# Loads and stores of a log-softmax moved into one DMA queue, one whole tile in turns

## The chip, the cores and the metric

The kernel runs on one core of one Trainium2 chip. The metric is the device time of one execution in microseconds (us). Where this document speaks of packets, a "row" is a contiguous run of 50,000 bytes (a quarter of a row of the array), which is what one packet of a whole-tile transfer moves, and the "excess" is the time by which a packet is longer than the shortest usual one, 1847 ns.

## The reference

A log-softmax over the last axis of a float32 array of 16 x 512 x 50,000:

```python
max_x = np.max(x, axis=-1, keepdims=True)
shifted = x - max_x
log_sum_exp = np.log(np.sum(np.exp(shifted), axis=-1, keepdims=True))
return (shifted - log_sum_exp).astype(np.float32)
```

Every byte is read once and written once: 1638.4 MB each way.

## The kernel before

The 8192 rows of the array are cut into 256 tiles of 32 rows; a tile is 128 partitions of 12,500 floats (6.4 MB), four partitions to a row, and four buffers hold tiles in flight. SyncE issues the loads, ScalarE the stores, and each issuing engine owns one DMA queue. VectorE finds maxima and subtracts, ScalarE makes exponentials and their sums, and TensorE adds the sums of the four partitions of a row.

```python
    @block.sync                                   # loads
    def _(sync):
        ...
        load_parts(0, 0)                          # the first tile in four quarters
        for t in range(1, NBUF):
            load(t, xt[t])
        take(sync, stored[0], 16 * NS)
        load(0, xt[NBUF])
        src = run(xt, NBUF + 1, rounds - 1)
        with sync.Fori(0, rounds - 1) as q:
            for i in range(NBUF):
                j = (i + 1) % NBUF
                take(sync, stored[j])             # the buffer's store has landed
                load(j, src(q, i))
        ...
        load_parts(NBUF - 1, ntiles - 1)          # the last tile in quarters too

    @block.scalar                                 # exponentials, and the stores
    def _(scalar):
        ...
        def store(j, dst, buf):
            subtracted.next(scalar.dma_start(out=dst, in_=buf)).then_inc(stored[j], 16)

        def whole(j, dst):
            for c in range(NS):
                ...                               # exp of a quarter of the columns, with its sum
            ...
            log(j)
            store(j, dst, bufs[j])
```

Of the kernel before, what the change touches and what calls it, by code (L numbers as in the profile page):

```python
# [19 lines left out]
NBUF = 4  # L20

NS = 4
# [27 lines left out]
def cols(c):  # L50
    return slice(c * C, (c + 1) * C)
# [3 lines left out]
def kernel(  # L55
# [12 lines left out]

    rounds = (ntiles - NBUF) // NBUF
    assert ntiles % NBUF == 0 and rounds >= 2  # L70
    tail = range(1 + rounds * NBUF, ntiles - 1)

    xt = xf.rearrange("(t r) (g w) -> t (r g) w", r=R, g=G)
    ot = of.rearrange("(t r) (g w) -> t (r g) w", r=R, g=G)
# [63 lines left out]
    def _(gpsimd):  # L138
        k = 0
        for g in (GS, G):  # L140
# [10 lines left out]
            ).wait_op(ready, k + 2, "sem-ge").then_inc(ready)  # L151
            k += 3

    @block.sync
    def _(sync):
        def load(j, src):
            sync.dma_start(out=bufs[j], in_=src).then_inc(landed[j], 16)

        def load_parts(j, t):
            for s in range(NS):  # L160
                sync.dma_start(out=bufs[j][:, cols(s)], in_=xs[t, s]).then_inc(
                    landed_part[s], 16
                )

        load_parts(0, 0)
        for t in range(1, NBUF):
            load(t, xt[t])
        take(sync, stored[0], 16 * NS)
        load(0, xt[NBUF])
        src = run(xt, NBUF + 1, rounds - 1)  # L170
        with sync.Fori(0, rounds - 1) as q:
            for i in range(NBUF):
                j = (i + 1) % NBUF
                take(sync, stored[j])
                load(j, src(q, i))
        for t in tail:
            take(sync, stored[t % NBUF])
            load(t % NBUF, xt[t])
        take(sync, stored[NBUF - 1])
        load_parts(NBUF - 1, ntiles - 1)  # L180
        for j in range(NBUF - 1):
            take(sync, stored[j])
        take(sync, stored[NBUF - 1], 16 * NS)

    @block.vector
    def _(vector):
        def share(k, g, op, negate):

            on_dve.next(
                vector.transpose(out=allneg, in_=negp.to_broadcast([P, SQ]))  # L190
            ).then_inc(on_dve.sem)
            on_dve.next(
                vector.tensor_reduce(  # L193
                    out=rowneg[:, : SQ // g],
                    in_=allneg.rearrange("p (r g) -> p r g", g=g),
                    op=op, axis=AX, negate=negate,
                )
            ).then_inc(on_dve.sem)
            on_dve.next(
                vector.tensor_copy(  # L200
                    out=spread.rearrange("p (r g) -> p r g", g=g),
                    in_=rowneg[:, : SQ // g, None].to_broadcast([P, SQ // g, g]),
                )
            ).then_inc(on_dve.sem)
            on_dve.next(
                vector.transpose(out=negmaxs[k], in_=spread)  # L206
            ).then_inc(agreed.sem)

        def subtract(k, buf):
            logged.next(  # L210
                vector.tensor_scalar(  # L211
                    out=buf, in0=buf, scalar1=negmaxs[k][:, 0:1], scalar2=logs[k],
                    op0=ALU.add, op1=ALU.subtract,
                )
            ).then_inc(subtracted.sem)

        def whole(j):
            take(vector, landed[j])

            for c in range(NS):  # L220
                vector.tensor_reduce(  # L221
                    out=negms[j][:, c : c + 1], in_=bufs[j][:, cols(c)],
                    op=ALU.max, axis=AX, negate=True,
                ).then_inc(shifted.sem if c < NS - 1 else on_dve.sem)
            on_dve.next(vector.nop()).then_inc(shifted.sem)  # L225
            vector.tensor_reduce(  # L226
                out=negp, in_=negms[j], op=ALU.min, axis=AX
            ).then_inc(on_dve.sem)
            share(j, G, ALU.min, False)

            rescaled.next(
                vector.tensor_mul(out=scaleds[j], in0=scales[j], in1=parts[j])  # L232
            ).then_inc(summed.sem)
            subtract(j, bufs[j])

        def in_parts(j):
            for s in range(NS):
                take(vector, landed_part[s])
                vector.reduce_max(  # L239
                    out=negp, in_=bufs[j][:, cols(s)], axis=AX  # L240
                ).then_inc(on_dve.sem)
                share(NBUF + s, GS, ALU.max, True)
                if s:
                    subtract(NBUF + s - 1, bufs[j][:, cols(s - 1)])
            subtract(NBUF + NS - 1, bufs[j][:, cols(NS - 1)])

        def settle():
            for count in (on_dve, rescaled, logged):
                count.settle(vector)

        in_parts(0)
        settle()
        with vector.Fori(0, rounds):
            for i in range(NBUF):
                whole((i + 1) % NBUF)
            settle()
        for t in tail:
            whole(t % NBUF)
        in_parts(NBUF - 1)

    @block.scalar
    def _(scalar):
        def log(k):
            added.next(
                scalar.activation(out=logs[k], in_=rowsums[k], func=ACT.Ln)  # L265
            ).then_inc(logged.sem)

        def store(j, dst, buf):
            subtracted.next(scalar.dma_start(out=dst, in_=buf)).then_inc(stored[j], 16)

        def whole(j, dst):
            for c in range(NS):
                shifted.next(
                    scalar.activation(  # L274
                        out=dump, in_=bufs[j][:, cols(c)], func=ACT.Exp,
                        bias=negms[j][:, c : c + 1], scale=1.0,
                        accum_out=parts[j][:, c : c + 1],
                    )
                ).then_inc(on_act.sem)
                on_act.next(scalar.nop())  # L280
            agreed.next(
                scalar.activation(  # L282
                    out=scales[j], in_=negms[j], func=ACT.Exp,
                    bias=negmaxs[j][:, 0:1], scale=-1.0,
                )
            ).then_inc(rescaled.sem)
            log(j)
            store(j, dst, bufs[j])

        def in_parts(j, t):  # L290
            for s in range(NS):
                agreed.next(
                    scalar.activation(  # L293
                        out=dump, in_=bufs[j][:, cols(s)], func=ACT.Exp,
                        bias=negmaxs[NBUF + s][:, 0:1], scale=1.0,
                        accum_out=sub_sum[:, s : s + 1],
                    )
                ).then_inc(summed_part.sem)
                if s:
                    store(j, os[t, s - 1], bufs[j][:, cols(s - 1)])  # L300
                log(NBUF + s)
            store(j, os[t, NS - 1], bufs[j][:, cols(NS - 1)])

        def settle():
            for count in (on_act, shifted, agreed, added, subtracted):
                count.settle(scalar)

        nc.scalar.preload_act_table_set("natural_log_exp_and_others")  # L308
        in_parts(0, 0)
        settle()  # L310
        dst = run(ot, 1, rounds)
        with scalar.Fori(0, rounds) as q:
            for i in range(NBUF):
                whole((i + 1) % NBUF, dst(q, i))
            settle()
        for t in tail:
            whole(t % NBUF, ot[t])
        in_parts(NBUF - 1, ntiles - 1)

    @block.tensor  # L320
    def _(tensor):
        def whole(j):
            for c in range(NS):
                ins = tensor.matmul(  # L324
                    rowsums[j], ones[G], scaleds[j][:, c : c + 1],
                    start=c == 0, stop=c == NS - 1,
                )
                if c == 0:
                    summed.next(ins)
            ins.then_inc(added.sem)  # L330

        def in_parts():
            for s in range(NS):
                summed_part.next(
                    tensor.matmul(  # L335
                        rowsums[NBUF + s], ones[GS], sub_sum[:, s : s + 1],
                        start=True, stop=True,
                    )
                ).then_inc(added.sem)
            summed_part.settle(tensor)  # L340

        tensor.wait_ge(ready, 6)
        in_parts()
        with tensor.Fori(0, rounds):
            for i in range(NBUF):
                whole((i + 1) % NBUF)
            summed.settle(tensor)
        for t in tail:
            whole(t % NBUF)
        in_parts()  # L350


# [28 lines left out]
```

## Time and profile before

| | kernel before |
|---|---|
| time, median of the first 3 runs | 7594.52 us (7588.5 to 7618.48) |
| span of the profiled run | 7612.1 us |
| DMA queues | loads 50.2%, stores 49.8% of 16 engines |
| VectorE, ScalarE, TensorE busy | 72%, 42%, 6% |

The queue shares are the time that packets took on 16 DMA engines; they add up to the whole span. So transfers bind, and every microsecond must be looked for in the packets. The trace keeps a record of each packet (start, duration, size, queue, but not the engine's number). From these records come the packet means. The **trailing time** below comes from the landings that the trace keeps for each semaphore: a transfer ends with 16 of them, one per engine, and the trailing time is how much later the last one is than the median of the 16.

### The profile page before, as it was taken

To read this page: it belongs to the slowest core of one execution; us is meant where nothing else is said; L and a number is where in the kernel's file an instruction comes from. 1 tells how busy PE (TensorE), PEld (TensorE's weight loads), DVE (VectorE), ACT (ScalarE), POOL (GpSimd) and SP (SyncE) were. 2 spreads that over 40 slices of the span, in tenths; PEclk is the share of its full clock that TensorE was granted. 3 is DMA by queue.
4 is the path that set the end of the run, shared out by engine and by line. 5 is a ranking of instruction groups with operands and counts; after the bars stand their busy time and mean duration, and the time that the engine had idled before them with its cause. 6 is when DMAs were issued, how large, how long until landed. Compare 5 with 4: busy or idle time off the path is not lost. (4 is left out here: it accounts for less than half of the span.)

```text
span 7612.1 us, 14101 instructions
## 1 busy us (share of the span) xinstructions
PE 478.8 (6%) x2048; PEld 456.4 (6%) x2048; DVE 5445.7 (72%) x2842; ACT 3185.1 (42%) x2565; POOL 2.3 (0%) x10
## 2 busy tenths in 40 slices
PE   0000000000000000000000000000000000000000
PEld 0000000000000000000000000000000000000000
DVE  7777777777776777777767777777777777777777
ACT  4344444434444344443443444434434444344443
POOL 0000000000000000000000000000000000000000
DMA  9999999999999999999999999999999999999999
GB/s 423 434 433 433 434 434 434 433 433 434 434 433 432 432 432 431 431 432 428 429 429 429 426 427 429 431 430 432 432 431 431 433 433 433 434 433 431 432 433 393
DMA packets 75458, 3276.85 MB, mean 430 GB/s; under 512 B 8384, under 2 KB 8384, under 8 KB 8384
## 3 DMA queue, kind: packets, MB, share of 16 engines
q1 hardware_dynamic: 37728, 1638.42, 50.2%
q10 hardware_dynamic: 37728, 1638.42, 49.8%
q14 instruction: 2, 0.02, 0.0%
HBM read 1638.40 MB, written 1638.40 MB: 430 GB/s over the span
## 5 line engine op out<-in xcount | busy, mean ns | idle before, releaser
L274 ACT ACTIVATE dump<-buf,negm 128x3125 f32<-128x3125 f32 x1016 | 2914.3, 2868 | 3807.2 <-DVE negm L221 3710.5
L221 DVE TENSOR_REDUCE negm<-buf 128x1 f32<-128x3125 f32 x1016 | 3391.7, 3401 | 943.6 <-DVEq L47 943.6
L211 DVE TENSOR_SCALAR buf<-buf,negmax,logsum 128x12500 f32<-128x12500 f32 (+1 forms) x262 | 1739.7, 6640 | 553.9 <-ACT logsum L265 553.9
L324 PE MATMUL sums<-scaled,ones 128*128 128x1 f32 x2032 | 474.1, 355 | 7061.9 <-DVE scaled L232 7061.9
L324 PEld LDWEIGHTS sums<-scaled,ones 128*128 128x128 f32 x2032 | 452.4, 328 | 7083.6 <-DVE scaled L232 7083.6
L232 DVE TENSOR_TENSOR scaled<-scale,part 128x4 f32<-128x4 f32 x254 | 41.2, 162 | 575.4 <-ACT scale L282 575.4
L265 ACT ACTIVATE logsum<-sums 128x1 f32<-128x1 f32 x262 | 44.8, 171 | 552.3 <-PE sums L324 546.9
L274 ACT ACTIVATION_READ_ACCUMULATOR dump<-buf,negm 128x1 f32 x1016 | 189.4, 186 | 0.0
L282 ACT ACTIVATE scale<-negm,negmax 128x4 f32<-128x4 f32 x254 | 75.5, 297 | 23.5
L226 DVE TENSOR_REDUCE negp<-negm 128x1 f32<-128x4 f32 x254 | 39.9, 157 | 38.9 <-DVE negm L221 38.9
L206 DVE STREAM_TRANSPOSE negmax<-spread 128x32 f32<-128x32 f32 x262 | 55.5, 212 | 9.1
L190 DVE STREAM_TRANSPOSE allneg<-negp 128x32 f32<-128x32 f32 x262 | 55.4, 212 | 9.1
L193 DVE TENSOR_REDUCE rowneg<-allneg 128x8 f32<-128x32 f32 (+1 forms) x262 | 48.8, 186 | 9.1
L200 DVE COPY spread<-rowneg 128x32 f32<-128x32 f32 x262 | 47.5, 181 | 9.1
L293 ACT ACTIVATE dump<-buf,negmax 128x3125 f32<-128x3125 f32 x8 | 22.9, 2869 | 30.9 <-DVE negmax L206 30.9
L239 DVE TENSOR_REDUCE negp<-buf 128x1 f32<-128x3125 f32 x8 | 27.2, 3399 | 8.1 <-DVEq L47 8.1
L335 PE MATMUL sums<-sub_sum,ones 128*128 128x1 f32 x16 | 4.7, 363 | 59.0 <-ACT dump L293 59.0
L335 PEld LDWEIGHTS sums<-sub_sum,ones 128*128 128x128 f32 x16 | 4.0, 312 | 59.6 <-ACT dump L293 59.6
L308 ACT ACT_TABLE_LOAD x1 | 1.3, 1283 | 1.0 <-SPq L115 1.0
L293 ACT ACTIVATION_READ_ACCUMULATOR dump<-buf,negmax 128x1 f32 x8 | 1.5, 186 | 0.0
L144 POOL TENSOR_SCALAR_AFFINE_SELECT ones<-ones 128x128 f32<-128x128 f32 x2 | 0.9, 442 | 0.1
L148 POOL TENSOR_SCALAR_AFFINE_SELECT ones<-ones 128x128 f32<-128x128 f32 x2 | 0.9, 428 | 0.1
(5 smaller groups left out, 0.8 us busy)
## 6 DMA issues: line engine op xcount, KB each, us to landing
buf<-in_x_dram SPq DMA_DIRECT2D x254, 6250.0 KB, 39.9
out_dram<-buf ACTq DMA_DIRECT2D x254, 6250.0 KB, 52.6
buf<-in_x_dram SPq DMA_DIRECT2D x8, 1562.5 KB, 27.6
out_dram<-buf ACTq DMA_DIRECT2D x8, 1562.5 KB, 18.3
```

Source lines behind the costliest of these rows:

```text
L190: vector.transpose(out=allneg, in_=negp.to_broadcast([P, SQ]))
L193: vector.tensor_reduce(out=rowneg[:, : SQ // g], in_=allneg.rearrange("p (r g) -> p r g", g=g), op=op, axis=AX, negate=negate,)
L200: vector.tensor_copy(out=spread.rearrange("p (r g) -> p r g", g=g), in_=rowneg[:, : SQ // g, None].to_broadcast([P, SQ // g, g]),)
L206: vector.transpose(out=negmaxs[k], in_=spread)
L211: vector.tensor_scalar(out=buf, in0=buf, scalar1=negmaxs[k][:, 0:1], scalar2=logs[k], op0=ALU.add, op1=ALU.subtract,)
L221: vector.tensor_reduce(out=negms[j][:, c : c + 1], in_=bufs[j][:, cols(c)], op=ALU.max, axis=AX, negate=True,).then_inc(shifted.sem if c < ...
L226: vector.tensor_reduce(out=negp, in_=negms[j], op=ALU.min, axis=AX).then_inc(on_dve.sem)
L232: vector.tensor_mul(out=scaleds[j], in0=scales[j], in1=parts[j])
L265: scalar.activation(out=logs[k], in_=rowsums[k], func=ACT.Ln)
L274: scalar.activation(out=dump, in_=bufs[j][:, cols(c)], func=ACT.Exp, bias=negms[j][:, c : c + 1], scale=1.0, accum_out=parts[j][:, c : c + 1],
L282: scalar.activation(out=scales[j], in_=negms[j], func=ACT.Exp, bias=negmaxs[j][:, 0:1], scale=-1.0,)
L324: ins = tensor.matmul(rowsums[j], ones[G], scaleds[j][:, c : c + 1], start=c == 0, stop=c == NS - 1,)
```

## The change

The intent: one queue in place of two, so that the order of the transfers is the program's and no longer the engines' choice packet by packet. SyncE issues store t, waits until store t-1 has landed, and issues the load that reuses that buffer. The last tile, which came in quarters, is whole. The core of the diff:

```diff
-    tail = range(1 + rounds * NBUF, ntiles - 1)
+    tail = range(1 + rounds * NBUF, ntiles)
     ... (SyncE)
+        def store(t, dst):
+            j = t % NBUF
+            subtracted.next(sync.dma_start(out=dst, in_=bufs[j])).then_inc(stored[j], 16)
     ...
         with sync.Fori(0, rounds - 1) as q:
             for i in range(NBUF):
-                j = (i + 1) % NBUF
-                take(sync, stored[j])
-                load(j, src(q, i))
+                store(2 + i, dst(q, i))
+                take(sync, stored[(1 + i) % NBUF])
+                load(1 + i, src(q, i))
+            subtracted.settle(sync)
     ... (ScalarE)
-            store(j, dst, bufs[j])
     ... (VectorE, ScalarE and TensorE lose in_parts for the last tile)
```

More of the change, by code (lines that the diff above doesn't have):

```diff
@@ L155, in _, with load @@
     def _(sync):
-        def load(j, src):
+        def load(t, src):
+            j = t % NBUF
             sync.dma_start(out=bufs[j], in_=src).then_inc(landed[j], 16)
-        def load_parts(j, t):
-            for s in range(NS):
-                sync.dma_start(out=bufs[j][:, cols(s)], in_=xs[t, s]).then_inc(
-                    landed_part[s], 16
-                )
-        load_parts(0, 0)
+        def store(t, dst):
+            j = t % NBUF
+            subtracted.next(sync.dma_start(out=dst, in_=bufs[j])).then_inc(stored[j], 16)
+        for s in range(NS):
+            sync.dma_start(out=bufs[0][:, cols(s)], in_=xs[0, s]).then_inc(
+                landed_part[s], 16
+            )
         for t in range(1, NBUF):
             load(t, xt[t])
+        for s in range(NS):
+            subtracted.next(
+                sync.dma_start(out=os[0, s], in_=bufs[0][:, cols(s)])
+            ).then_inc(stored[0], 16)
+        store(1, ot[1])
         take(sync, stored[0], 16 * NS)
-        load(0, xt[NBUF])
-        src = run(xt, NBUF + 1, rounds - 1)
+        load(NBUF, xt[NBUF])
+        subtracted.settle(sync)
+        dst, src = run(ot, 2, rounds - 1), run(xt, NBUF + 1, rounds - 1)
         with sync.Fori(0, rounds - 1) as q:
             for i in range(NBUF):
-                j = (i + 1) % NBUF
-                take(sync, stored[j])
-                load(j, src(q, i))
-        for t in tail:
-            take(sync, stored[t % NBUF])
-            load(t % NBUF, xt[t])
-        take(sync, stored[NBUF - 1])
-        load_parts(NBUF - 1, ntiles - 1)
-        for j in range(NBUF - 1):
-            take(sync, stored[j])
-        take(sync, stored[NBUF - 1], 16 * NS)
+                store(2 + i, dst(q, i))
+                take(sync, stored[(1 + i) % NBUF])
+                load(1 + i, src(q, i))
+            subtracted.settle(sync)
+        for t in range(2 + NBUF * (rounds - 1), ntiles):
+            store(t, ot[t])
+            take(sync, stored[(t - 1) % NBUF])
+            if t + NBUF - 1 < ntiles:
+                load(t + NBUF - 1, xt[t + NBUF - 1])
+        take(sync, stored[(ntiles - 1) % NBUF])
     @block.vector
@@ L258, in _ @@
             whole(t % NBUF)
-        in_parts(NBUF - 1)
     @block.scalar
@@ L266, in log, with whole @@
             ).then_inc(logged.sem)
-        def store(j, dst, buf):
-            subtracted.next(scalar.dma_start(out=dst, in_=buf)).then_inc(stored[j], 16)
-        def whole(j, dst):
+        def whole(j):
             for c in range(NS):
@@ L287, in whole, with in_parts @@
             log(j)
-            store(j, dst, bufs[j])
-        def in_parts(j, t):
+        def in_parts(j):
             for s in range(NS):
@@ L298, in in_parts @@
                 ).then_inc(summed_part.sem)
-                if s:
-                    store(j, os[t, s - 1], bufs[j][:, cols(s - 1)])
                 log(NBUF + s)
-            store(j, os[t, NS - 1], bufs[j][:, cols(NS - 1)])
         def settle():
-            for count in (on_act, shifted, agreed, added, subtracted):
+            for count in (on_act, shifted, agreed, added):
                 count.settle(scalar)
         nc.scalar.preload_act_table_set("natural_log_exp_and_others")
-        in_parts(0, 0)
+        in_parts(0)
         settle()
-        dst = run(ot, 1, rounds)
-        with scalar.Fori(0, rounds) as q:
+        with scalar.Fori(0, rounds):
             for i in range(NBUF):
-                whole((i + 1) % NBUF, dst(q, i))
+                whole((i + 1) % NBUF)
             settle()
         for t in tail:
-            whole(t % NBUF, ot[t])
-        in_parts(NBUF - 1, ntiles - 1)
+            whole(t % NBUF)
     @block.tensor
@@ L349, in _ @@
             whole(t % NBUF)
-        in_parts()
 _INS = ['x']
```

## The prediction

> **What bounds the kernel now.** I read the page's DMA rows first, then its queue table, then the groups of instructions, and last the stretches of the trace at both ends of the run.
>
> ```profile
> DMA  9999999999999999999999999999999999999999
> GB/s 423 434 433 433 434 434 434 433 433 434 434 433 432 432 432 431 431 432 428 429 429 429 426 427 429 431 430 432 432 431 431 433 433 433 434 433 431 432 433 393
> DMA packets 75458, 3276.85 MB, mean 430 GB/s; under 512 B 8384, under 2 KB 8384, under 8 KB 8384
> q1 hardware_dynamic: 37728, 1638.42, 50.2%
> q10 hardware_dynamic: 37728, 1638.42, 49.8%
> ```
>
> All 40 slices have the 16 DMA engines at 90% or more, and the two queues together fill 100.0% of their time: q1 (SyncE, loads) and q10 (ScalarE, stores) move 1638.42 MB each. So the transfers are the bound, and the reader should ask only two things: how far the rate is from its best, and where an engine has nothing to do. The compute engines have room:
>
> ```profile
> L274 ACT ACTIVATE dump<-buf,negm 128x3125 f32<-128x3125 f32 x1016 | 2914.3, 2868 | 3807.2 <-DVE negm L221 3710.5
> L221 DVE TENSOR_REDUCE negm<-buf 128x1 f32<-128x3125 f32 x1016 | 3391.7, 3401 | 943.6 <-DVEq L47 943.6
> L211 DVE TENSOR_SCALAR buf<-buf,negmax,logsum 128x12500 f32<-128x12500 f32 (+1 forms) x262 | 1739.7, 6640 | 553.9 <-ACT logsum L265 553.9
> ```
>
> The 943.6 us ahead of the maxima on VectorE is its wait for a landed tile: 943.6 / 252 = 3.7 us per tile. In the timeline at 3020 us the maxima of one tile start at 3020.06, its store is issued at 3046.07 and the next store at 3075.6 or so: 26.0 us of work in a period of 29.6 us. The period is two transfers of 6.4 MB: 12.8 MB / 29.6 us = 432 GB/s, or 14.8 us for each transfer.
>
> The trace's single packet records give the rate its floor. A row of 50,000 bytes has a median of 1847 ns in both directions, and the next packet of the same engine starts 4 ns before it ends: 1843 ns of pitch, 27.1 GB/s per engine, 434 GB/s for 16. The excess is small and lies in the loads: they average 1864 ns (6.6% of them over 1870 ns), stores 1848 ns. The packet that sets a semaphore costs 9 ns.
>
> At the end of the run there is a hole:
>
> ```profile
> 7550.00:7560.00 10.00, 0.00 (x0) 0.00 (x0) 10.00 (x4) 6.42 (x5) 0.00 (x0) 1.00 0.99 428
> 7560.00:7570.00 10.00, 1.87 (x8) 1.78 (x8) 5.27 (x8) 6.02 (x6) 0.00 (x0) 1.00 0.43 185
> 7570.00:7575.00 5.00, 0.00 (x0) 0.00 (x0) 5.00 (x1) 0.00 (x0) 0.00 (x0) 1.00 0.13 55
> 7575.00:7580.00 5.00, 0.00 (x0) 0.00 (x0) 4.86 (x7) 0.25 (x1) 0.00 (x0) 1.00 0.79 340
> ```
>
> The last two columns are the DMA share and GB/s. From about 7563 to 7575 us a share of 0.13 means that two of 16 engines work: 14 have emptied both queues while VectorE finishes the tile before the last, and two that fell about 13 us behind are still at it. So the hole costs the 14 quick engines about 12 us and the slowest ones next to nothing.
>
> **What the Trainium skill says.** "DMA: Bandwidth & Descriptors", section "Issuing engines are not separate DMA queues": DMAs of any issuer run on the same 16 engines and interleave, and a second issuer saves only issue time. The trace agrees: an issue takes 0.33 us on SyncE's queue and 0.34 us on ScalarE's, against 14.8 us of data. Same page, section "Queues, rings and completion order": each engine takes turns between its queues packet by packet, and within a ring takes descriptors in order. The trace shows exactly that, one load row and one store row in turns wherever both queues have work. Same page, section "Where 436 GB/s comes from": 435.2 GB/s as the ceiling of the 16 ports; 434 from the pitch is as good as there. "HBM Reference", section "Specifications (TRN2)": a core that streams alone measures about 425 GB/s. The mixed stream here is above it (433 to 434 in the good slices), so a mixed stream isn't worse than a pure one by that page.
>
> **The change, part by part.**
> 1. *Stores move from ScalarE's queue to SyncE's.* 262 issues of 0.34 us leave ScalarE, 89 us in all on an engine 42% busy: nothing. SyncE issues 518 in place of 262, of 0.33 us: 171 us of 7600, nothing.
> 2. *Whole transfers in turns in one ring.* The order becomes L(t), S(t-2), L(t+1), S(t-1), L(t+2), S(t). From the landing of L(t) to the start of S(t) lie four transfers, 4 x 14.8 = 59 us; the work needs 26 us and some 2 us of signalling. SyncE's waiting for the subtraction therefore doesn't empty the ring. L(t+3) is issued when S(t-1) is through, with L(t+2) and S(t) still ahead: 29.6 us of queued work. I find no idle time in the steady state. The landing times should be near 44 us for loads (three transfers from issue) and near 46 us for stores (59 + 14.8 - 28).
> 3. *Start.* Loads of tiles 0 to 3 take 4 x 14.8 = 59 us after about 2.9 us. The parts of tile 0 are ready at about 35 us and tile 1 at about 61 us, before the ring reaches them at 62 and 77 us: no hole.
> 4. *End.* After L(255) lands, S(253) and S(254) remain ahead of S(255): 29.6 us, against about 28 us for the last tile. The 12 us hole closes, within a microsecond or two, though the last tile is now whole. For the slowest engine, which sets the end, the gain is only some 0 to 5 us.
> 5. *Packets.* Per engine, 2 x 255 x 8 = 4080 whole rows in place of 4064, and 64 quarter rows (464 ns of pitch) in place of 128: 4080 x 1.843 + 64 x 0.464 = 7549 us, plus about 3 us for 518 semaphore packets: 7552. The kernel before gives 7552 too. So the change in packet count is worth nothing.
>
> The sum: 7552 us, 2.9 us before the first packet, about 5 us from the last packet to the end, the excess of loads. For the kernel before the excess is 2032 x 0.017 + 2032 x 0.0014 = 37 us, and 7552 + 37 + 8 = 7597, plus about 11 us by which the slowest engine trails the mean: 7608, against a span of 7612.1. The unprofiled median is 7594.5. With the same excess the changed kernel comes to about 7590 to 7595.
>
> **The rivals.** What stays open is the excess of loads when all 16 engines read at once for 14.8 us and then all write, in place of a mixture.
> - *Rival A, the mixture causes the excess and it goes away.* For it: in the opening, 422 quarter rows loaded with no store beside them, after the first microseconds, average 468.6 ns with a floor of 468, and the excess is nearly all in loads that share engines with stores. Then 7552 + 8 = 7560 us, with a trailing engine 7565: 0.4% faster, and the floor of any version of these bytes.
> - *Rival B, pure reading is worse.* For it: the first whole-tile load has packets of 1881 to 2242 ns in its second row, some of which had started before the first store moved; 103 rows in that stretch average 1962 ns, 6% above the floor. Against it: the following 91 rows average 1848 ns. If 2 to 3% of the loads' 2040 x 1.847 = 3768 us stayed, 75 to 113 us, the time would be 7635 to 7675; with 6% throughout, 7790.
> - *Rival C, one ring drains between a load and a store.* A drain of 0.5 us at each of 510 turns would add 255 us. Against it: in the opening the engines pass from part to part of the same ring 6 ns after the semaphore packet starts. But a store's semaphore followed by more work of the same ring is what the old trace doesn't show in the steady state. I give this little weight.
>
> **Range and chances.** Between "as before" (7592), Rival A (7565) and a mild Rival B (7640), I choose 7600 us. The low end is just above the floor of 7560; the high end takes Rival B at 2 to 3%. Faster by over 2% would be under 7446, below the floor of 7552 of pure packets: 1%, for what I can't see. Slower by over 2% is over 7746: 6% or drains needed throughout; I say 5%. The rest, 94%, is within 2%.
>
> **What would show each step.** Right: one queue with all 3277 MB and nearly 100%; ScalarE's queue gone; landings near 44 and 46 us for whole loads and stores; VectorE's busy time unchanged near 5446 us; no slice at the end with a DMA share under 0.5 before the last store. The mean of a load's packet decides between A (1848 ns) and B (1885 to 1905 or more). Slices with a low DMA share in mid-run, or stores waiting for SyncE, would show step 2 wrong; gaps of some 100 ns after semaphore packets would show C. A time above 7680 or a hole in each period would make this prediction wrong.

## The result, and the profile after

The changed kernel takes 7593.84 us (median of 6 runs, 7593.22 to 7596.08); the kernel before, with more runs beside it, 7582.07 us (6 runs, 7571.15 to 7618.48). The ratio is 1.001 with a 95% interval of 0.9988 to 1.0032: the same. Ratios here are the mean time of one kernel's fast runs over that of the other's of the same rounds, so not quite the ratio of the medians.

The page of the changed kernel, the rows that answer to those shown of before; first the DMA rows and queues, then two groups of instructions, then the issues:

```profile
DMA  9999999999999999999999999999999999999999
GB/s 423 430 433 433 432 433 433 433 433 433 433 432 434 433 433 432 434 432 434 432 432 434 433 433 432 434 434 433 432 434 434 431 433 434 433 433 433 434 433 391
q1 hardware_dynamic: 74592, 3276.83, 100.0%
...
L279 ACT ACTIVATE dump<-buf,negm 128x3125 f32<-128x3125 f32 x1020 | 2925.8, 2868 | 3790.2 <-DVE negm L230 3693.0
L230 DVE TENSOR_REDUCE negm<-buf 128x1 f32<-128x3125 f32 x1020 | 3405.0, 3400 | 915.3 <-DVEq L47 915.3
...
buf<-in_x_dram SPq DMA_DIRECT2D x255, 6250.0 KB, 44.2
out_dram<-buf SPq DMA_DIRECT2D x255, 6250.0 KB, 48.0
```

One queue holds everything and is full. Before, the rate fell to between 426 and 429 GB/s in seven slices of mid-run; now it is 431 to 434 in all slices but the first two and the last. VectorE still waits for landed tiles (915.3 us), so transfers still bind. A whole load takes 44.2 us from issue to landing and a store 48.0, with two other transfers ahead of each.

The waits of SyncE's own queue after the change (waiter, releaser, us in total, times, longest):

```profile
SPq L47 <- SPq L47: 4588.9, 256, 19.1
SPq L164 <- DVE buf L220: 2690.6, 255, 25.5
```

A reader may take 2690.6 us of stores waiting for the subtraction as a loss. It isn't: SyncE waits 10.6 us per store while the ring behind it still holds work, and the DMA row shows no gap.

The end of the changed kernel (stretch, its length, busy time of TensorE, its weight loads, VectorE, ScalarE and GpSimd with counts, clock, DMA share, GB/s):

```profile
7550.00:7560.00 10.00, 0.00 (x0) 0.00 (x0) 10.00 (x4) 8.79 (x6) 0.00 (x0) 1.00 0.94 405
7560.00:7570.00 10.00, 1.86 (x8) 1.78 (x8) 5.28 (x8) 3.64 (x6) 0.00 (x0) 1.00 0.07 30
7570.00:7580.00 10.00, 0.00 (x0) 0.00 (x0) 3.09 (x1) 0.00 (x0) 0.00 (x0) 1.00 0.77 330
```

The hole at the end is still there. A share of 0.07 is one engine of 16 (0.0625): 15 engines have nothing to do while VectorE works on the last tile, and one is still busy with the store before it. By the landing records this engine runs 16 us behind the others here: it ends the last load at 7547.0 us, the median engine at 7530.7, and only then can VectorE start. It has no hole of its own, and ends the last store at 7591.6 us, the others at about 7589.2.

### The profile page after: what moved, and what is told of

It is laid out like the page before. It is cut to its first block, busy times and chain, and to the rows that moved or that the text cites. A ratio compares the mean times of both kernels' runs of the same rounds, so it can differ in the third digit from the quotient of the medians.

```text
span 7593.1 us, 13885 instructions
## 1 busy us (share of the span) xinstructions
PE 478.3 (6%) x2048; PEld 456.1 (6%) x2048; DVE 5442.9 (72%) x2829; ACT 3184.9 (42%) x2563; POOL 2.3 (0%) x10
## 5 line engine op out<-in xcount | busy, mean ns | idle before, releaser
L230 DVE TENSOR_REDUCE negm<-buf 128x1 f32<-128x3125 f32 x1020 | 3405.0, 3400 | 915.3 <-DVEq L47 915.3
## 6 DMA issues: line engine op xcount, KB each, us to landing
buf<-in_x_dram SPq DMA_DIRECT2D x255, 6250.0 KB, 44.2
```

The lines of the kernel that those rows point to most:

```text
L230: vector.tensor_reduce(out=negms[j][:, c : c + 1], in_=bufs[j][:, cols(c)], op=ALU.max, axis=AX, negate=True,).then_inc(shifted.sem if c < ...
```

## The experiments

Theory 1: a ring in which all engines go in the same direction has a small constant excess per packet, and two mixed rings have one that comes and goes from run to run; so the change trades one for the other. Rivals: the end decides (the whole last tile costs what the queue gained), or the chip decides (the numbers shift with the session).

### The changed kernel again, in two sessions

No edit. 

> The changed kernel again, on one chip with the kernel before. Theory 1 (one ring puts all engines in the same direction and leaves a small, constant excess of about 3 ns in each 50,000-byte packet, while the mixture of two queues has an excess that comes and goes from run to run): 7590 to 7597 us in every run, with a spread under 6 us, while the kernel before spreads over 20 us or more. Rival (the two kernels differ by the chip they happened to run on): the spread of both is alike, under 10 us, and their ratio is the same in every session.

> The changed kernel in a second session, beside the kernel before in the same rounds. Theory 1: 7590 to 7597 us again with a spread under 6 us, and the kernel before anywhere from 7570 to 7620 us. Rival (the chip decides): both shift together.

Measured: 7595.01 us (5 runs, 7593.24 to 7595.97) beside 7582.46 for the kernel before (11 runs, 7573.1 to 7624.59), ratio 1.0013 (0.9991 to 1.0035); then 7594.59 us (6 runs, 7593.57 to 7595.6) beside 7586.79 (11 runs, 7571.1 to 7614.79), ratio 1.0012 (0.9994 to 1.0029). The changed kernel stays within 3 us in 17 timed runs of three sessions, the kernel before spreads over 44 to 52 us inside one session. The rival of the chip falls. The 0.1% in the ratio isn't clear of zero in any session, because of the spread of the kernel before. All three sessions together give means of 7594.5 us (17 runs) and 7587.3 us (28 runs): 7 us more for the changed kernel, with about 1 to 13 us as a 95% interval. If this is real, it is a loss of 0.1%, far below the 2% that counts.

### The end alone: two queues with a whole last tile

```diff
 # from the kernel before
-    tail = range(1 + rounds * NBUF, ntiles - 1)
+    tail = range(1 + rounds * NBUF, ntiles)
-        load_parts(NBUF - 1, ntiles - 1)          # and in_parts on the other engines
+        # the last tile is loaded, worked and stored whole
```

> The kernel before with its last tile whole in place of in quarters, still two queues: the end alone is changed. Theory 1: the end is worth only some microseconds and the time follows the kernel before, 7565 to 7620 us, with its spread. Rival (the whole last tile costs what the one queue gained): 10 to 20 us above the kernel before in the same rounds, near 7590 to 7595.

Measured: 7578.58 us (6 runs, 7569.7 to 7617.36), ratio to before 0.9994 (0.997 to 1.0019). It has the spread of the kernel before and about its median. So no cost of the end can be seen, though the interval still allows some 14 us, and what separates the two kernels' spread is the queue. The next run tests the end in the kernel with the small spread.

### The other half: one queue with the last tile in quarters

```diff
 # from the changed kernel: the last tile is loaded, worked and stored in quarters
+        for s in range(NS):
+            subtracted.next(
+                sync.dma_start(out=os[last, s], in_=bufs[NBUF - 1][:, cols(s)])
+            ).then_inc(stored[NBUF - 1], 16)
```

> The changed kernel with its last tile in quarters as before: the other half of the same separation. If the slowest DMA engine has work up to the last store, as the trace of the changed kernel suggests, the end is bound by it and the time stays at 7590 to 7596 us. Rival: the hole before the last store (about 13 us in 15 of 16 engines) is on the path, and filling it brings 7578 to 7585 us.

Measured: 7596.81 us (5 runs, 7595.63 to 7599.56), some 2 us above the changed kernel of the same rounds, and just above the 7590 to 7596 us expected. Its last stretches:

```profile
7560.00:7570.00 10.00, 0.58 (x2) 0.50 (x2) 9.19 (x12) 5.46 (x4) 0.00 (x0) 1.00 0.84 358
7570.00:7580.00 10.00, 0.59 (x2) 0.50 (x2) 1.91 (x1) 0.87 (x3) 0.00 (x0) 1.00 1.01 424
7580.00:7585.00 5.00, 0.00 (x0) 0.00 (x0) 0.00 (x0) 0.00 (x0) 0.00 (x0) 1.00 0.43 183
7585.00:7590.00 5.00, 0.00 (x0) 0.00 (x0) 0.00 (x0) 0.00 (x0) 0.00 (x0) 1.00 0.07 28
```

The hole from 7560 to 7570 us is filled (0.84 in place of 0.07), and a new one stands at the very end: again one engine of 16 works alone, from about 7583 us. The time of the hole moved behind the other engines' last store. The trailing engine sets the end, and the hole was never on its path.

### The ring emptied once per tile

```diff
                 take(sync, stored[(1 + i) % NBUF])
+                sync.wait_ge(stored[(2 + i) % NBUF], 16)
                 load(1 + i, src(q, i))
```

> The changed kernel with one wait more: each load waits also for the store issued just before it, so that the ring is empty once per tile. It measures what step 2 of the prediction says the change avoids. If an emptied ring costs [...]3 to 4.5 us per tile for 252 tiles: 8350 to 8740 us. If the ring was never filled ahead in the changed kernel (step 2 wrong), little changes: under 7700 us.

Measured: 8733.72 us (one look). Its DMA rows and the wait on SyncE's queue:

```profile
GB/s 396 370 377 376 374 377 371 378 373 367 377 378 372 378 374 374 377 370 370 374 370 371 377 378 381 374 371 369 373 374 370 378 377 374 378 368 372 376 372 403
q1 hardware_dynamic: 74592, 3276.83, 92.2%
```

```profile
SPq L160 <- DMA out_dram<-buf: 8194.3, 248, 34.3
```

The added wait stands in the loop and runs 248 times. The span grew by 8732.0 - 7593.1 = 1139 us, 4.6 us for each of 248 tiles. The queue's share of 92.2% leaves 7.8% of 8732, 681 us, in which engines have nothing: 2.7 us per tile, somewhat below the 3 to 4.5 expected. The rest is in the packets: rows average 1964 ns in place of 1851.5, and summed over an engine's rows their excess is 477 us in place of 18. 681 + 459 = 1140 us, the whole difference. The records put nearly all of this excess in two of the 16 rows that an engine moves per tile: the first after the restart (2608 ns on average) and one that starts 13 to 15 us later, near the turn from load to store (2955 ns). What makes them long wasn't separated further. The time lies just inside the expected range, but only because the longer rows came on top of the idle time: in that, the expectation was lucky. So the two transfers queued ahead in the changed kernel are worth 15% of the time.

### Reading alone, writing alone

```diff
 # reading alone: from the changed kernel, wrong result on purpose
-            subtracted.next(sync.dma_start(out=dst, in_=bufs[j])).then_inc(stored[j], 16)
+            subtracted.next(sync.dma_start(out=bufs[j], in_=dst)).then_inc(stored[j], 16)   # dst: the same tile of x
 # writing alone: from the changed kernel, wrong result on purpose
-                load(1 + i, src(q, i))
+                load2(1 + i, src(q, i))          # a store of the buffer to the tile src of out
```

> One queue, each store replaced by a second load of the same tile into the same buffer; the result is wrong on purpose, the bytes moved are the same. It measures pure reading by itself. Rival A of the prediction (reading alone has no excess): 7560 to 7575 us, packets near 1847 ns. Theory 1 (a small constant excess in any pure phase): 7580 to 7600 us, packets near 1850 ns. Rival B (pure reading is worse than a mixture by 2 to 3%): over 7635 us, packets of 1885 ns or more.

> One queue, each load after the first four tiles replaced by a store of the same size; the result is wrong on purpose. Pure writing by itself. If the small excess comes from all engines writing at once: packets of 1850 ns or more and 7585 us or more. If writing alone has none: 1847 ns and 7560 to 7570 us.

Measured, one look each: 7580.18 us for reading alone, 7632.7 us for writing alone. Rows average 1851.0 and 1854.6 ns. Reading alone:

```profile
GB/s 424 432 433 433 433 433 433 433 433 433 433 432 433 433 433 433 433 433 433 433 433 433 433 433 433 433 433 433 433 433 433 433 433 433 433 433 433 433 433 420
```

The rate is flat at 433 GB/s from the third slice on. Reading alone has the constant 4 ns of Theory 1, and no trace of a loss of 2 to 3%: Rival B of the prediction falls. Its engines stay together, too: trailing time 2.8 us near the end.

In writing alone one engine falls behind, by up to 28.6 us, and the others keep within 1 us of their median. The packet records can be sorted by engine after all, because the next packet of an engine starts within some ns of the end of the one before. Sorted so, the slow engine's rows average 1864.2 ns, an excess of 70 us in all, and those of the other 15 average 1854.0. The slow engine works from 2.8 us to 7629 us of the 7631.0 us span with 0.5 us of idle time, so it alone makes the time: 7552 + 70 and some 5 us for the two ends are within 4 us of the span. The other 15 stand idle for 41 us each, 26 of them in the last 80 us:

```profile
7550.00:7600.00 50.00, 1.86 (x8) 1.78 (x8) 37.15 (x21) 22.69 (x17) 0.00 (x0) 1.00 0.72 312
7600.00:7631.00 31.00, 1.87 (x8) 1.78 (x8) 6.96 (x2) 2.18 (x4) 0.00 (x0) 1.00 0.51 218
```

So falling behind belongs to stores. The changed kernel shows the same inside one run: from 2500 to 5900 us its trailing engine has loads of 1850 ns like the others, and stores of 1859 to 1860 ns against 1850 to 1851.

### Reading alone through two rings

```diff
 # from the kernel before, wrong result on purpose: ScalarE's queue loads the same tile again
-            store(j, dst, bufs[j])
+            store(j, bufs[j], dst)               # out=bufs[j], in_= the tile of x
```

> The kernel before with its stores of whole tiles replaced by second loads on ScalarE's queue (wrong result on purpose): two rings in turns, but one direction. It tells whether the constant 4 ns per packet of the loads-only run (mean 1851 ns, 7580 us) come from one direction or from one ring. One direction: a mean of 1850 ns or more. One ring: 1847 to 1848 ns and 7562 to 7570 us.

Measured: 7581.69 us (one look). Rows average 1851.4 ns on one queue and 1850.1 on the other. Two rings in turns, one direction, and the constant excess is there: for loads it comes with the single direction and not with the single ring. Stores through two rings weren't tried.

### Tiles in another order

```diff
+    def real(t):
+        return (t + half) % ntiles               # tiles 128..255, then 0..127
-            store(t, ot[t])
+            store(t, ot[real(t)])                # and so for all loads and stores
```

> The changed kernel with tiles taken in the order 128 to 255, then 0 to 127; the same bytes and the right result. In the changed kernel one DMA engine falls behind between 2400 and 6000 us (by some 9 us; tiles 81 to 203) and keeps pace before and after. If the addresses decide: it falls behind from the start to 2200 us and again from 6200 us on, and keeps pace between. If the time or the engine decides: again between 2400 and 6000 us. The total stays at 7590 to 7600 us either way.

Measured: 7594.41 us (one look). The trailing time, from the landing records of the semaphores (not a view of the profile):

```
trace's clock, us    594   1895  2546  3196  3847  4497  5148  5798  6449  7099
changed kernel       2.5   2.3   3.7   5.3   6.8   8.5  10.3  12.0  13.3  15.0
rotated tiles        2.6   2.3   3.7   5.4   7.1   9.4  10.9  12.5  14.1  15.7
reading alone        2.0   2.2   2.3   2.4   2.5   2.6   2.7   2.8   2.8   2.8
writing alone        2.9  11.3  15.6  19.7  24.0  28.2  28.3  28.3  28.4  28.4
```

The same engine-behind-the-pack curve appears at the same times with other tiles, so the addresses don't decide. The curve rises by about 1.6 us in 650 us and doesn't stop: it reaches 16.4 us in the store before the last, and 16.9 us with rotated tiles. The part of the expectation by which the engine keeps pace after 6000 us is wrong. That reading came from counting semaphore packets sixteen by sixteen in order of time, which puts an engine's packet into the wrong transfer once it is nearly one transfer (14.8 us) late. Writing alone does stop, at 28.4 us. That is just under the two transfers (29.6 us) that SyncE queues ahead, and from there on the other engines have idle time. In two more traces of the changed kernel the rise starts up to some 600 us later and ends at 15.4 and 15.7 us. The records don't name engines; why one is slower in stores, and why it starts when it does, stays open.

### The kernel before, a second trace

No edit. 

> The kernel before, for a second trace of it. Theory 1: stretches without any excess (434 GB/s) and stretches with 1 to 2% of it, at other times than in the first trace, so the time differs from run to run. Rival (the addresses decide): the same slices, 18 to 30 of 40, are slow again.

Measured: 7572.3 us (one look), against 7613.83 for its first profiled run; another run of the same kernel in the same session took 7599.36 us.

```profile
GB/s 423 435 432 435 434 432 435 433 434 435 432 434 434 432 435 433 434 435 432 434 434 432 435 433 434 435 432 435 434 432 435 432 434 435 432 435 434 433 435 406
```

None of the slow slices of the first trace is there, though the kernel moves the same tiles in the same order: they go with the run, not with the data. Loads average 1847.9 ns and stores 1847.2. What this run loses lies largely at its end:

```profile
7540.00:7550.00 10.00, 0.00 (x0) 0.00 (x0) 2.60 (x1) 0.00 (x0) 0.00 (x0) 1.00 0.84 350
7550.00:7560.00 10.00, 0.58 (x2) 0.50 (x2) 9.33 (x12) 4.87 (x4) 0.00 (x0) 1.00 0.41 173
7560.00:7571.00 11.00, 0.58 (x2) 0.50 (x2) 1.95 (x2) 1.45 (x3) 0.00 (x0) 1.00 0.69 291
```

The missing shares of these stretches add up to 11 us of idle time per engine, more than half of the 19 us by which its span of 7570.6 us lies above the floor of 7552.

Put side by side (excess: the sum over all whole rows, divided by 16 engines):

| run | time, us | excess per engine, us |
|---|---|---|
| two queues, first trace | 7613.83 | 37.3 |
| two queues, second trace | 7572.3 | 2.3 |
| two queues, whole last tile | 7617.36 | 40.5 |
| one queue, three traces | 7594.8, 7595.01, 7594.57 | 18.3, 19.4, 18.8 |
| one queue, rotated tiles | 7594.41 | 17.8 |
| reading alone, one ring / two rings | 7580.18 / 7581.69 | 16.3 / 15.1 |

Theory 1 holds as far as it says what happens to the packets. It leaves out the trailing engine: the changed kernel takes 14 us more than reading alone with only 2 us more of excess, and most of the rest is that its slowest engine is 15 to 16 us behind and not 3. What starts an excess in a mixed run, and why one direction costs 4 ns a row, was not found. No version came out that clearly beats both kernels; the best runs of the kernel before, at 7571 us, are 19 us above the floor of 7552 us of pure packets.

## Why the prediction was right

The time lies in the stated range, 6 us from the predicted 7600, and in the class foretold. By its own steps:

1. *Issues cost nothing:* right. VectorE is busy for 5442.9 us and ScalarE for 3184.9, as before, and SyncE's 518 issues leave no mark in the DMA row.
2. *The ring stays filled:* right. Loads land after 44.2 us where 44 was worked out, stores after 48.0 where 46 was. The emptied ring shows what being wrong here would have cost: 1139 us.
3. *The start:* right, as far as it reaches: once the first packets have come, at 3 us, no slice of 1.5 us in the first 60 us has a DMA share under 0.6, and 31 of the 40 are at 0.9.
4. *The end:* wrong in the picture, right in the worth. "The 12 us hole closes, within a microsecond or two" didn't happen: from 7560 to 7570 us the DMA share is 0.07. I had counted the queued work of an engine in step with the slowest. But the last load has landed only when the slowest engine has it, 16 us after the median, and by then the other 15 have only some 13 of their 29.6 us of queued work left, against 28 us for the last tile: they stand idle for 14 us. That the slowest gains next to nothing was right, and the quarter-tile end shows it: the hole filled, the time 2 us longer.
5. *Packets:* the floor of 7552 us stands, and no run came below it.

*The rivals.* Of the excess I gave 1848 ns per load for Rival A and 1885 to 1905 for B. Measured are 1851.5 ns over loads and stores together: far from B, and nearer to A, with 18 us in place of 37. But A's cause doesn't hold: a mixed run can have 2 us of excess, so the mixture alone doesn't make it, and with the mixture gone the excess didn't go away. A direction has a small excess of its own, and stores have it too: rows that start well inside one direction, away from the turns, average about 1850 ns for loads and 1850 to 1851 ns for stores. Rival C, the drain at each turn, falls: in the changed kernel's records the next row starts 6 ns after a semaphore packet starts, in the median and in over 95% of cases, after loads and stores alike.

*The sum, as measured:* 7552 + 18 of excess + 4 for both ends + about 15 by which the trailing engine is behind the mean = 7589 us, against a span of 7593.1; 4 us are not placed. For the ends I had counted 8, with "about 5 us from the last packet to the end"; the records show the first packet at 2.0 us and the end of the last one 2.0 us before the span's end. The excess is 19 us less than "as before". The trailing time is 15 in place of 11, and the lag of "about 13 us" that I read off the kernel before was too small: near 7500 us three of its engines are 14, 17 and 30 us behind the median. That the total still came out within 6 us owes something to luck: these terms are small and partly cancel.

One thing the prediction took for fixed and wasn't: "the unprofiled median is 7594.5" was one draw. Over the later sessions the same kernel runs from 7571 to 7625 us, and its two traces have an excess of 2 and of 37 us. The expected gain of Rival A (37 us of excess) was thus partly a gain over a bad run: the session medians of the kernel before, 7582 to 7587 us, already lie below the changed kernel.

## What to carry to other kernels

When the DMA engines are full, work out the packets' floor first (rows times the pitch of a row), since it caps every gain for the same packets; changing who issues a transfer, and in which order, could here move only the time above it. Merging the queues was safe here because the ring held two transfers ahead of each wait; then the waits on the issuing engine, some 7280 us in all, cost nothing; with the ring emptied once per tile the time grew by 15%. Look at each engine's lag and not only at the mean of 16: a tile is there only when the slowest engine has brought its share. Take several traces before explaining a slow stretch: here one kernel's slow slices went away in its next run, and a hole in 15 of 16 engines wasn't on the path because the sixteenth had none.

## What the Trainium skill lacked or had wrong

- "DMA: Bandwidth & Descriptors", section "Where 436 GB/s comes from", says that for transfers between HBM and SBUF the HBM side at about 358 GB/s binds; the sentence lacks the condition, given elsewhere on the page, that the other core of the pair streams too. On one core running alone every version with a filled ring went at 426 to 435 GB/s in mid-run, whether it loaded, stored or did both, just under the ceiling of 435.2 given there.
- The same page, section "Latency and other measured facts", puts slower DMA engines down to descriptor rings of the software path, as a best guess, and calls it specific to that path. All transfers here go the hardware path, and still one engine fell 14 to 17 us behind the median in every trace of the one-queue kernels that load and store with a filled ring, and 28 us when only storing, with rows of 1864 ns against 1854. Which engine, the trace doesn't tell.
- No page has what mixing directions costs or gains: rows of 1847 to 1848 ns in a good mixed run, 1851 ns reading alone, 1855 ns writing alone (1854 without its slow engine), and loads of 1864 to 1866 ns in a bad mixed run, with the time from 7571 to 7625 us for one kernel.
- No page has the price of an emptied hardware ring for transfers of 6.4 MB: 4.6 us per tile here, 2.7 of them idle and 1.9 in two longer rows.
